# A two-layer decoder trunk on one core: the entry into the second FFN, and the order in which attention copies its accumulators out

## The chip, the cores and the metric

One Trainium2 chip; the program runs on one of its cores. The metric is the time of one execution on the device in microseconds (us). Runs of the kernel before give 2144.81, 2145.89 and 2146.08 us, median 2145.89 us. "Before axis" times below are microseconds from the start of the span in the profiled execution of the kernel before.

## The reference

The trunk has two layers of width 1024 over 1024 positions. Each layer is a mixer and a dense SwiGLU feed-forward part (FFN), each with an RMS norm ahead of it and a residual addition behind it.

```python
for i in range(DEPTH):                       # DEPTH = 2
    h = rms_norm(x, mix_norm[i])
    if i % 2 == 0:
        x = x + short_conv_mixer(h, ...)
    else:
        x = x + dilated_attention_mixer(h, ...)   # 16 heads x 64, 3 dilated branches
    h = rms_norm(x, ffn_norm[i])
    x = x + swiglu(h, w_gate, w_up, w_down)  # (silu(h @ w_gate) * (h @ w_up)) @ w_down
return rms_norm(x, final_norm)
```

Everything is fp32. The RMS norm needs, for each position, the mean over 1024 features of the squares.

## The kernel before

**Numbers and layout.** The residual x lies transposed in SBUF as eight tiles `X[k]` of 128 features x 1024 positions; "first half" and "second half" are columns 0 to 511 and 512 to 1023. An fp32 operand is used as two parts: ScalarE (ACT) copies it to the rounded type fp32r (the high part; L139 for weights, L567 for FFN operands), VectorE (DVE) subtracts that from the operand (the low part; L140, L568). A product is then three matmuls on TensorE (PE): high x high, high x low, low x high. The weight splits stand in one list; `ensure(i)` makes all splits up to number i at that point of the program, `take` hands one out.

**Order.** The order of each engine's instructions is the order in which the program writes them (`manual_schedule`, L103); an engine that waits holds back all that stands behind it. PSUM has eight banks of 128x512, handed out in a ring; a new accumulation waits until what was copied or read from its bank is done.

**FFN.** The FFN's in-projection is done with Strassen's products: a unit (u, m) is product m (1 to 7) of output block u, 12 matmuls of 128x512 each (L575 to L577). `unit_order` (L262) writes the order; in the second FFN (`key` 1) it is, by number n from 0: (0,1) (1,1) (2,1) (3,1) (0,2) (1,2) (2,2) (3,2) (4,1) (4,2) (0,6) (1,6) (0,7) (1,7) (0,4) (1,4) (0,5) (1,5) (0,3) (1,3) (2,6) (2,5) (2,7) (3,6) and so on. `save` (L581) is ACT's copy of a partial from its bank into an SBUF tile `part`; `add` (L585) is DVE's addition of a bank to such a part. `whole` (L613) calls them, and `out` (L1235) finishes a quarter of the output: even units (gate) through Silu on ACT (L1239), odd units (up) by DVE's product with the gate (L1242), then a store from the POOL queue (L741) and, when all four quarters of a block are there, four DVE sums (L749). The quarter (0,0) of blocks 0 to 3 needs only products 1 and 2; `first` adds the bank of product 2 to the part of product 1. Before, the four quarters (0,0) of blocks 0 to 3 are finished behind unit (0,4), number 14.

**The second operand set.** Products 3 to 7 need sums and differences of normalised halves. `second_half` (L1187 and around it) is a generator whose steps make four DVE combinations, or four high parts on ACT (L567) and four low parts on DVE (L568). `feed_forward` calls its steps behind certain unit numbers, `n in (5, 6, 9, 10, 11, 15)` for the second FFN (L1273).

**Entering the FFN.** The attention's out-projection ("ao") produces X[k], first half for k = 0 to 7, then second half for k = 0 to 7, nine matmuls each on lines L369 to L371. DVE adds each bank to X[k] (L506), and `chained` (L448) sums the squares for the norm: ACT squares X[k] (L460 or L467); the sum over k is made in one of two ways. With `by_dma` (the first FFN's norm) k = 0 goes to `acc`, k = 1 to `acc2`, k = 2 to 5 are added by four accumulating DMAs from the POOL queue (L469, even k onto `acc`, odd k onto `acc2`), and DVE adds the square of k = 6, then `acc2`, then the square of k = 7 (L470). Without it (the second FFN's norm) DVE adds all seven (L462). `put_off` holds an addition back by one step. `stats` (L485 to L502) turns the sums into the scale of each position: PE sums over features, ACT a root (L488), DVE a reciprocal and a diagonal (L489, L494), PE spreads it (L501), ACT copies it out (L502). Between the k's, `gained` (L1179, L1183) scales the second half by the gain on ACT and adds four tiles by accumulating DMAs on the POOL queue; ACT's queue spills X[k] to HBM (L1331); SP's queue loads weights (L151).

**Attention.** Heads are worked in pairs p, two heads a. `values` (L1566 on) accumulates output and denominator of one head in two banks, `acc[0]` for the first and `acc[1]` for the second column half. In a loop of j = 0 to 7 ACT copies the denominators (L1598) and outputs (L1599) of `acc[0]` out behind j = 3, of `acc[1]` behind j = 7. Scores (L1503, L1504) of a later head take the freed banks. `finish` (L1601) of the last pair takes logarithm and exponential of the denominators (L1631), multiplies (L1624) and splits the outputs for the out-projection, half by half; the weight splits of the out-projection, 128x384 each ("ao"), follow.

Of the kernel before, what the change touches and what calls it, by code (L numbers as in the profile page):

```python
# [24 lines left out]
NPAIR = H // 2  # L25
# [70 lines left out]
def trunk(ctx: ExitStack, tc: tile.TileContext, x, gains_in, cwi, ck, cwo, wqkv, wo, relb,  # L96
# [8 lines left out]
    def page(name, dt=F32):  # L105
        return pages.tile([128, 1024], dt, name=name, tag="page", bufs=PAGES)
# [3 lines left out]
    def half_page(name, dt=F32):  # L110
        return scope["pool"].tile([128, 512], dt, name=name, tag="half", bufs=scope["halves"])
# [4 lines left out]
    def half(h):  # L116
        return slice(h * HALF, (h + 1) * HALF)
# [45 lines left out]
    def ensure(upto):  # L163
        while op_state[0] < min(upto + 1, len(ops)):
            key = ops[op_state[0] + 1][0] if op_state[0] + 1 < len(ops) else None
            if key in sums_of:
                sums_of.pop(key)()
            if op_state[0] not in made:
                made[op_state[0]] = ops[op_state[0]][1]()
            op_state[0] += 1  # L170
# [223 lines left out]
    class Norm:  # L394
# [57 lines left out]
        def chained(self, k, c0, c1):  # L452

            s = slice(c0, c1)
            if self.acc is None:
                self.acc, self.rstd = page("acc"), page("rstd")
            acc = self.acc[:, s]
            if not self.by_dma and k:
                to = half_page("sq")
                nc.scalar.activation(to, X[k][:, s], AF.Square)  # L460
                self.flush()
                self.put_off = lambda: nc.vector.tensor_tensor(out=acc, in0=acc, in1=to, op=ALU.add)  # L462
                return
            if k == 1:
                self.odd = half_page("acc2")
            to = half_page("sq") if k > 1 else self.odd if k else acc
            nc.scalar.activation(to, X[k][:, s], AF.Square)  # L467
            if 1 < k < 6:
                nc.gpsimd.dma_start(out=(acc, self.odd)[k % 2], in_=to, accum_op=ALU.add)  # L469
            add = lambda t: nc.vector.tensor_tensor(out=acc, in0=acc, in1=t, op=ALU.add)  # L470
            if k > 5:
                self.put_off = lambda: add(to)
            if k == KT - 2:
                self.flush()
                add(self.odd)
                self.odd = None
# [64 lines left out]
    class Strassen:  # L541
# [75 lines left out]
        def whole(self, u, m, d):  # L617

            if m == 1:
                d["p"] = self.bank()  # L620
            elif m in (2, 5):
                d["q" if m == 2 else "r"] = self.bank()
            self.mm((u,), m, d["q" if m == 2 else "r" if m in (5, 3) else "p"], m in (1, 2, 5))
            if m in (1, 6, 7):
                d[{1: "u1", 6: "u2", 7: "u3"}[m]] = self.save(d["p"])
            if (u, m) == (0, 6):
                self.first(0)
            if m == 4:
                self.out(u, (1, 0), d.pop("p"))
            elif m == 3:  # L630
                self.out(u, (0, 1), self.add(d.pop("u2"), d.pop("r")))
            elif m in (5, 7) and "u3" in d and "r" in d:
                self.out(u, (1, 1), self.add(d.pop("u3"), d["r"]))
            early = self.key != 0
            if m == 2 and u > 3 + early or (u, m) in ((0, 4), (3, 7)):
                for x in {0: range(4), 3: (4,) * early}.get(u, (u,)):
                    self.out(x, (0, 0), self.first(x))
                    del self.st[x]["u1"]

# [506 lines left out]
    class Swiglu(Strassen):  # L1146
# [100 lines left out]
        def feed_forward(self, stats, last_step, after, final=None):  # L1247
            prep = []

            def start(n):  # L1250
                if n == 0:
                    last_step()
                    if not self.key:
                        for m in (6, 7):
                            combos[self.key, 1](m)
                        ensure(self.at(3, 1))
                if n == 1 + self.key:
                    next(stats)
                if n == 1:
                    if self.key:  # L1260
                        for m in (6, 7):
                            combos[self.key, 1](m)
                    ensure(self.at(0, 6))
                if n == 2 + 2 * self.key:
                    run(stats)
                    prep.append(self.second_half())
                    next(prep[0])
                    nc.scalar.activation(scratch, eps, AF.Silu)
                if n == 2:
                    ensure(self.at(1, 6))  # L1270
                elif n == 4:
                    ensure(self.at(1, 7))
                if n in ((5, 7, 8, 9, 11), (5, 6, 9, 10, 11, 15))[self.key]:  # L1273
                    ensure(self.base + n + 3)
                    next(prep[0], None)

            self.run(start)
            key = ("d", self.key)
            if final:
                final(key, self.plain, self.hid)  # L1280
                return
            for n in range(KT):
                add_to_x(n, both(take(key + (n,)), self.plain, self.hid))
                after(n)
# [98 lines left out]
    def attention(norm):  # L1383
# [185 lines left out]
        def values(p, a, st):  # L1569
            lf, lh, ld, lp = (st[n] for n in ("lf", "lh", "ld", "lp"))  # L1570
            o, z = st["o"], st["z"]
            n0 = slice(64 * a, 64 * a + 64)
            z0 = slice(64 - 64 * a, 128 - 64 * a)
            acc = [bank(), bank()]
            kd = [[128, 4], [1, 32]]
            b1 = [[32, 16], [1, 8]]

            def mm(ih, off, dims, u, rhs, first=False, last=False):
                nc.tensor.matmul(view(acc[ih], off, dims), vx[:, u, 64 * a:64 * a + 128], rhs,  # L1579
                                 start=first, stop=last)  # L1580

            for ih in range(2):
                for r4 in range(4):
                    mm(ih, r4 * 32, kd, 8 + r4, view(lf, ih * HALF + r4 * 32, kd), first=r4 == 0)
                    if r4 % 2:
                        yield
            for r4 in range(4):
                mm(1, r4 * 32, kd, 12 + r4, view(lh, r4 * 32, kd))
                if r4 % 2:
                    yield  # L1590
            for j in range(8):
                off = (j % 4) * 8
                mm(j // 4, off, b1, j, view(ld, blk(j), b1), last=False)
                if j:
                    mm(j // 4, off, b1, j - 1, view(lp, blk(j), b1), last=j % 4 == 3)
                if j % 4 == 3:
                    ih, s = j // 4, half(j // 4)
                    nc.scalar.activation(z[n0, s], acc[ih][z0], AF.Copy)  # L1598
                    nc.scalar.activation(o[n0, s], acc[ih][n0], AF.Copy)  # L1599
                yield  # L1600

        def finish(p):

            o, z = OZ.pop(p)
            if p < NPAIR - 1:
                zd, rd = zdram[p]
                nc.sync.dma_start(zd, z[0:65:64])
                yield
                zc = scope["pool"].tile([128, 16], F32, name="zc", tag="zc", bufs=2)
                nc.sync.dma_start(zc, bass.AP(zd.tensor, zd.offset, [[16, 128], [1, 16]]))  # L1610
                yield
                nc.vector.reciprocal(zc, zc)
                nc.sync.dma_start(bass.AP(rd.tensor, rd.offset, [[16, 128], [1, 16]]), zc)
                yield
                nc.sync.dma_start(z, bass.AP(rd.tensor, rd.offset, [[S, 2], [0, 64], [1, S]]))
                yield
                put_off.append((p, o, z))
                return

            acts[p] = page("o_hi", F32R), page("o_lo", F32R)  # L1620

            def scaled(c0, c1):
                q = slice(c0, c1)
                nc.vector.tensor_tensor(out=o[:, q], in0=o[:, q], in1=z[:, q], op=ALU.mult)  # L1624

            def parts(h):
                split(o[:, half(h)], [t[:, half(h)] for t in acts[p]])

            nc.scalar.activation(z, z, AF.Ln)
            for h in range(2):  # L1630
                nc.scalar.activation(z[:, half(h)], z[:, half(h)], AF.Exp, scale=-1.0)  # L1631
                scaled(h * HALF, h * HALF + HALF)
                parts(h)
                yield

        def attended():
# [119 lines left out]
        ahead_ao = [k for k, f in ops].index(("ao", 1, 2))  # L1756
# [230 lines left out]
```

## Time and profile before

| what | value |
|---|---|
| runs, median | 2144.81, 2145.89, 2146.08; 2145.89 us |
| profiled execution, its own time | 2144.39 us |
| its span | 2142.6 us (1.79 us of the time lie outside it) |
| mean granted PE clock | 0.997 |
| busy PE / DVE / ACT / POOL | 2120.2 / 1728.1 / 1002.8 / 221.9 us |
| share of the span PE / DVE / ACT / POOL | 99% / 81% / 47% / 10% |
| busy share of the DMA queues: SP and plain hardware queue q1, POOL's software queue q0, ACT's hardware queue q10 | 30.2% / 10.5% / 3.0% |

A matmul's row shows a duration of 0.39 us for 128x512 while the next starts 0.227 us later, since matmuls overlap; a stall is therefore read as the distance of two starts less 0.227. In a row of a timeline stand start, duration, engine, line, operation, written tile and read tile, and in brackets the idle time ahead of it and what ended that. "x4" is a run of four alike, with its whole length.

### The profile page before, as it was taken

To read this page: it belongs to the slowest core of one execution; us is meant where nothing else is said; L and a number is where in the kernel's file an instruction comes from. 1 tells how busy PE (TensorE), PEld (TensorE's weight loads), DVE (VectorE), ACT (ScalarE), POOL (GpSimd) and SP (SyncE) were. 2 spreads that over 40 slices of the span, in tenths; PEclk is the share of its full clock that TensorE was granted. 3 is DMA by queue.
4 is the path that set the end of the run, shared out by engine and by line. 5 is a ranking of instruction groups with operands and counts; after the bars stand their busy time and mean duration, and the time that the engine had idled before them with its cause. 6 is when DMAs were issued, how large, how long until landed. Compare 5 with 4: busy or idle time off the path is not lost.

```text
span 2142.6 us, 30734 instructions
## 1 busy us (share of the span) xinstructions
PE 2120.2 (99%) x11086; PEld 1816.1 (85%) x11086; DVE 1728.1 (81%) x3160; ACT 1002.8 (47%) x1798; POOL 221.9 (10%) x316
## 2 busy tenths in 40 slices
PE   9999999999999999999999999999899999999998
PEld 7788887888888888878999999887788888888887
DVE  8898669888888788864777777868888888978886
ACT  7433336344544444344555555536544444444435
POOL 2000001111212000010111111110011212100000
PEclk9999999999999999999999999999999999999999
DMA  7222643335545784331333333635114544586432
GB/s 214 69 93 69 236 147 94 114 123 172 168 154 181 267 305 141 107 135 52 92 93 94 93 95 83 204 119 185 44 69 156 184 157 166 172 333 217 155 94 79
DMA packets 148067, 306.71 MB, mean 143 GB/s; under 512 B 49851, under 2 KB 61131, under 8 KB 147915
## 3 DMA queue, kind: packets, MB, share of 16 engines
q1 hardware_dynamic: 82026, 206.83, 30.2%
q0 software_dynamic: 25872, 79.02, 10.5%
q10 hardware_dynamic: 40016, 18.90, 3.0%
q8 instruction: 88, 1.44, 0.3%
q14 instruction: 65, 0.52, 0.1%
HBM read 209.06 MB, written 88.28 MB: 139 GB/s over the span
## 4 chain that ended last, share of the span: by engine, by line
PE 77%; issue 10%; DVE 7%; ACT 4%; DMA 2%; POOL 0%; SPq 0%; ACTq 0%; DVEq 0%; POOLq 0%
PE bank L575 16%; PE bank L576 16%; PE bank L577 16%; PE bank L1579 4%; PE bank L371 4%; PE bank L369 4%; PE bank L370 4%; PE bank L670 2%; PE bank L673 2%; PE bank L672 2%; PE bank L1504 1%; PE bank L1503 1%; PE bank L1444 1%; PE bank L1443 1%; PE bank L1442 1%
## 5 line engine op out<-in xcount | busy, mean ns | idle before, releaser
L575 PE MATMUL bank<-b,w 128*128 128x512 f32 x1816 | 710.2, 391 | 6.8 <-ACT part L581 2.8
L576 PE MATMUL bank<-b,w 128*128 128x512 f32 x1816 | 708.1, 390 | 0.5 <-DVE b L916 0.5
L577 PE MATMUL bank<-b,w 128*128 128x512 f32 x1816 | 707.5, 390 | 0.8 <-DVE w L140 0.8
L575 PEld LDWEIGHTS bank<-b,w 128*128 128x128 f32 x1816 | 341.5, 188 | 80.4 <-ACT part L581 3.7
L577 PEld LDWEIGHTS bank<-b,w 128*128 128x128 f32 x1816 | 341.3, 188 | 73.1 <-DVE w L140 1.9
L576 PEld LDWEIGHTS bank<-b,w 128*128 128x128 f32 x1816 | 341.4, 188 | 70.8 <-DVE b L916 1.4
L139 ACT ACTIVATE w<-combo 128x512 fp32r<-128x512 f32 (+2 forms) x448 | 229.1, 540 | 248.6 <-DVE combo L191 227.3
L140 DVE TENSOR_TENSOR w<-combo,w 128x512 fp32r<-128x512 f32 (+2 forms) x448 | 254.8, 582 | 31.5 <-ACT w L139 31.2
L581 ACT ACTIVATE part<-bank 128x512 f32<-128x512 f32 x168 | 100.0, 597 | 294.9 <-PE bank L577 291.2
L140 DVE TENSOR_TENSOR w<-raw,w 128x512 fp32r<-128x512 f32 (+2 forms) x308 | 169.4, 569 | 21.8 <-ACT w L139 21.6
L585 DVE TENSOR_TENSOR part<-part,bank 128x256 f32<-128x256 f32 (+1 forms) x328 | 154.2, 501 | 37.9 <-ACT part L581 21.5
L139 ACT ACTIVATE w<-raw 128x512 fp32r<-128x512 f32 (+2 forms) x308 | 150.8, 527 | 63.2 <-DMA raw<-in_ffn_w_down 18.5
L831 DVE TENSOR_TENSOR x<-x,bank 128x512 f32<-128x512 f32 x168 | 114.8, 684 | 37.1 <-PE bank L577 34.5
L369 PE MATMUL bank<-w_hi,w 128*128 128x512 f32 (+1 forms) x320 | 119.6, 374 | 0.0
L371 PE MATMUL bank<-w_hi,w 128*128 128x512 f32 (+1 forms) x320 | 117.9, 369 | 1.3 <-DVE w L140 1.3
L370 PE MATMUL bank<-w_lo,w 128*128 128x512 f32 (+1 forms) x320 | 117.8, 368 | 0.0
L506 DVE TENSOR_TENSOR x<-x,bank 128x512 f32<-128x512 f32 (+1 forms) x104 | 66.0, 643 | 55.9 <-PE bank L371 48.6
L369 PE MATMUL bank<-h_hi,w_hi 128*128 128x512 f32 x256 | 104.5, 408 | 0.0
L191 DVE TENSOR_TENSOR combo<-raw 128x512 f32<-128x512 f32 (+1 forms) x160 | 103.2, 645 | 0.0
L371 PE MATMUL bank<-h_hi,w_lo 128*128 128x512 f32 x256 | 100.0, 391 | 0.2 <-DVE w_lo L140 0.2
L370 PE MATMUL bank<-h_lo,w_hi 128*128 128x512 f32 x256 | 99.9, 390 | 0.0
L1557 POOL PARTITION_ALL_REDUCE mb<-m x16 | 51.6, 3222 | 395.1 <-DVE m L1554 325.7
(266 smaller groups left out, 3804.4 us busy)
## 6 DMA issues: line engine op xcount, KB each, us to landing
hin<-part SPq DMA_DIRECT2D x126, 256.0 KB
raw<-in_ffn_w_gate SPq DMA_DIRECT2D x44, 512.0 KB
raw<-in_ffn_w_up SPq DMA_DIRECT2D x44, 512.0 KB
b<-ready SPq DMA_DIRECT2D x42, 512.0 KB
part<-sum POOLq DMA_DIRECT2D x72, 256.0 KB, 3.5
raw<-in_ffn_w_down SPq DMA_DIRECT2D x48, 384.0 KB
x<-spill SPq DMA_DIRECT2D x24, 512.0 KB
raw<-in_attn_w_qkv SPq DMA_DIRECT2D x24, 512.0 KB
```

What stands on the lines that cost most here:

```text
L139: nc.scalar.activation(hi, src, AF.Copy)
L140: eng.tensor_tensor(out=lo, in0=src, in1=hi, op=ALU.subtract)
L191: eng.tensor_tensor(out=c, in0=a, in1=b, op=op)
L369: nc.tensor.matmul(b, whi[:, a], ahi[:, s], start=first, stop=False)
L370: nc.tensor.matmul(b, whi[:, a], alo[:, s], start=False, stop=False)
L371: nc.tensor.matmul(b, wlo[:, a], ahi[:, s], start=False, stop=last)
L575: nc.tensor.matmul(b, hi[:, a], bhi, start=start and k == 0, stop=False, skip_group_check=True)
L576: nc.tensor.matmul(b, hi[:, a], blo, start=False, stop=False, skip_group_check=True)
L577: nc.tensor.matmul(b, lo[:, a], bhi, start=False, stop=k == n - 1, skip_group_check=True)
L581: nc.scalar.activation(t, b, AF.Copy)
L585: nc.vector.tensor_tensor(out=t, in0=t, in1=b, op=ALU.add)
L831: nc.vector.tensor_tensor(out=X[n][:, half(h)], in0=X[n][:, half(h)], in1=b, op=ALU.add)
```

## The change

Five edits, all between the attention and the first third of the second FFN:

1. `chained`: for the second FFN's norm the second column half (c0 not 0) takes the branch of the accumulating DMAs; the first half keeps DVE's additions.
2. `whole`: in the second FFN the quarters (0,0) of blocks 0 to 3 are finished behind unit (1,3), number 19, and not behind (0,4), number 14.
3. `feed_forward`: the steps of `second_half` in the second FFN come behind numbers 5, 6, 11, 12, 13, 16 and no more behind 5, 6, 9, 10, 11, 15. The `ensure` beside it moves along.
4. `values`: for all pairs but the last both banks are copied out behind j = 7, `acc[1]` first, then `acc[0]`.
5. `finish`: the split of the fourth "ao" weight is made between the two halves of the last pair's outputs, and not behind both.

```diff
-            if not self.by_dma and k:
+            if not self.by_dma and k and not c0:
...
-            if m == 2 and u > 3 + early or (u, m) in ((0, 4), (3, 7)):
-                for x in {0: range(4), 3: (4,) * early}.get(u, (u,)):
+            if m == 2 and u > 3 + early or (u, m) in ((1, 3) if self.key == 1 else (0, 4), (3, 7)):
+                for x in {u * (u < 2): range(4), 3: (4,) * early}.get(u, (u,)):
...
-                if n in ((5, 7, 8, 9, 11), (5, 6, 9, 10, 11, 15))[self.key]:
+                if n in ((5, 7, 8, 9, 11), (5, 6, 11, 12, 13, 16))[self.key]:
...
-                if j % 4 == 3:
-                    ih, s = j // 4, half(j // 4)
+                for ih in ((j // 4,) * (j % 4 == 3) if p == NPAIR - 1 else (1, 0) * (j == 7)):
+                    s = half(ih)
                     nc.scalar.activation(z[n0, s], acc[ih][z0], AF.Copy)
                     nc.scalar.activation(o[n0, s], acc[ih][n0], AF.Copy)
...
                 parts(h)
+                if h == 0:
+                    ensure(ahead_ao + 1)
```

DVE's order at the end of the second column half of the out-projection (the last steps of `chained`, k = 6 and 7); `acc_13662` is the page `acc2`:

```order
 L506 TENSOR_TENSOR x<-x,bank 128x512
-L462 TENSOR_TENSOR acc<-acc,sq 128x512
+L470 TENSOR_TENSOR acc<-acc,sq 128x512
+L470 TENSOR_TENSOR acc<-acc,acc_13662 128x512
 L1157 SCALAR_TENSOR_TENSOR hcol<-x,gains,rstd 128x512
 L568 TENSOR_TENSOR b<-hcol,b 128x512
 L506 TENSOR_TENSOR x<-x,bank 128x512
-L462 TENSOR_TENSOR acc<-acc,sq 128x512 x2
+L470 TENSOR_TENSOR acc<-acc,sq 128x512
 L1157 SCALAR_TENSOR_TENSOR hcol<-x,gains,rstd 128x512
```

One addition in each of the steps of k = 2 to 5 above these rows is gone as well; here stand additions that read the square made just ahead of them and the page that the DMAs write.

ACT's order behind unit number 9 of the second FFN; `part<-bank` is `save`, `b<-hcol` a step's four high parts:

```order
 L567 ACTIVATE b<-x 128x512 x4
-L581 ACTIVATE part<-bank 128x512
+L581 ACTIVATE part<-bank 128x512 x3
+L139 ACTIVATE w<-raw 128x512
 L567 ACTIVATE b<-hcol 128x512 x4
-L581 ACTIVATE part<-bank 128x512 x2
-L139 ACTIVATE w<-raw 128x512
+L581 ACTIVATE part<-bank 128x512
+L139 ACTIVATE w<-raw 128x512
+L581 ACTIVATE part<-bank 128x512
+L139 ACTIVATE w<-combo 128x512
 L567 ACTIVATE b<-hcol 128x512 x4
```

The four high parts that stood ahead of two copies of partials now stand behind them, and so does the next group.

ACT's order in the attention, where one pair's second head ends; `w_hi<-raw` is a weight split of 128x640:

```order
 L1566 ACTIVATE lp<-lp 128x512
-L139 ACTIVATE w_hi<-raw 128x640
-L1598 ACTIVATE z<-bank 64x512
-L1599 ACTIVATE o<-bank 64x512
-L139 ACTIVATE w_hi<-raw 128x640
+L139 ACTIVATE w_hi<-raw 128x640 x2
+L1598 ACTIVATE z<-bank 64x512
+L1599 ACTIVATE o<-bank 64x512
 L1598 ACTIVATE z<-bank 64x512
 L1599 ACTIVATE o<-bank 64x512
```

The first pair of copies moves down to the second; all four stand together.

## The prediction

> **What bounds the kernel now.** The page first. PE is busy for all but 22 us of the span, so an edit is worth only the PE stalls that it takes away or makes.
>
> ```profile
> span 2142.6 us, 30734 instructions
> PE 2120.2 (99%) x11086; PEld 1816.1 (85%) x11086; DVE 1728.1 (81%) x3160; ACT 1002.8 (47%) x1798; POOL 221.9 (10%) x316
> ```
>
> Next PE's waits, asked for one stretch at a time: attention (960 to 1440), out-projection (1440 to 1480), end of the norm (1480 to 1520), first third of the second FFN (1520 to 1560). Columns: what waited, for whom, us in all, times, longest.
>
> ```profile
> PE bank L1503 <- ACT o L1599: 2.3, 4, 0.6
> ...
> PE bank L371 <- DVE w L140: 1.0, 1, 1.0
> ...
> PE bank L501 <- DVE diag L494: 0.9, 1, 0.9
> ...
> PE bank L575 <- ACT part L581: 2.8, 2, 1.5
> PE bank L575 <- DVE part L585: 1.9, 1, 1.9
> ```
>
> These nine stalls, 8.9 us, are what the five edits aim at. The last stretch costs more than its waits, as the table by windows shows (length, busy PE, PEld, DVE, ACT, POOL; granted clock, DMA share, GB/s):
>
> ```profile
> 1520.00:1560.00 40.00, 35.30 (x147) 28.08 (x146) 36.44 (x59) 19.79 (x35) 3.31 (x6) 0.96 0.09 34
> ```
>
> The clock is 0.96 there. PE's timeline has the place:
>
> ```profile
> 1544.67 0.39 PE L577 MATMUL bank<-b,w 128*128 128x512 f32 x1
> 1546.93 0.47 PE L575 MATMUL bank<-b,w 128*128 128x512 f32 x1 [1.87 <-DVE part L585]
> ...
> 1548.01 0.63 PE L576 MATMUL bank<-b,w 128*128 128x512 f32 x1
> ...
> 1551.34 0.39 PE L575 MATMUL bank<-b,w 128*128 128x512 f32 x1
> ```
>
> The first pair is a stall of 1546.93 - 1544.67 - 0.23 = 2.03 us (0.23 is the distance of two starts in full flow, as between the unit's other matmuls). Behind it eight matmuls take 1551.34 - 1548.01 = 3.33 us where 8 x 0.23 = 1.84 were due: 1.5 us more. So this stall cost 3.5.
>
> **Copies of accumulators (edit 4).** One of the four stalls on PE:
>
> ```profile
> 1072.04 0.40 PE L371 MATMUL bank<-h_hi,w_lo 128*128 128x512 f32 x1
> 1073.02 0.39 PE L1503 MATMUL bank<-qa,ka 128*128 128x256 f32 x1 [0.58 <-ACT o L1599]
> ```
>
> 0.98 - 0.23 = 0.75 us each, 3.0 for four. Freeing the banks in the other order changes which bank the scores get; I take it that all four go. But ACT now makes two pairs of copies where one stood. What a pair takes, and whether that hurts, is read in a slot and behind it:
>
> ```profile
> 1047.73 0.60 ACT L1598 ACTIVATE z<-bank 64x512 f32<-64x512 f32 x1 [2.23 <-PE bank L1579]
> 1048.34 0.59 ACT L1599 ACTIVATE o<-bank 64x512 f32<-64x512 f32 x1
> 1048.83 0.62 ACT L1472 ACTIVATE ka<-kq 64x512 fp32r<-64x512 f32 x1
> ...
> 1062.29 1.05 ACT L1566 ACTIVATE lf<-lf 128x1024 f32<-128x1024 f32 x1
> ...
> 1063.62 1.05 PE L1579 MATMUL bank<-lf,vx 128*128 128x128 f32 x8
> ...
> 1105.93 0.63 ACT L1472 ACTIVATE qb<-kq 64x512 fp32r<-64x512 f32 x1 [1.39 <-POOL mb L1557]
> ```
>
> A pair is 1048.83 - 1047.73 = 1.1 us, and the next head's operands (L1472) start that much later. In this slot ACT has no idle time from there to the exponential, which ends at 1063.34, 0.28 ahead of the PE that reads it; less some 0.06 from end to start, 0.2 of 1.1 is free and 0.9 becomes a stall. In the next slot ACT waits 1.39 on POOL, which swallows the 1.1. I found three slots of the first kind (the copies near 1048, 1155, 1262): 3 x 0.88 = -2.6. Sum **+0.4**, between 0 (one slot more) and +3.0 (DVE's or POOL's share of the chain hides it).
>
> **The "ao" split (edit 5).**
>
> ```profile
> 1459.78 0.39 PE L370 MATMUL bank<-w_lo,w 128*128 128x512 f32 x1
> 1461.15 0.50 PE L371 MATMUL bank<-w_hi,w 128*128 128x512 f32 x1 [0.98 <-DVE w L140]
> ...
> 1458.74 0.69 DVE L140 TENSOR_TENSOR o_lo<-o,o_hi 128x512 fp32r<-128x512 f32 x1 [0.70 <-ACT o_hi L139]
> ```
>
> PE lost 1.37 - 0.23 = 1.14, and 0.1 in the slower start of the next matmul. The split's low part fits into DVE's wait of 0.70 ahead of the second `o_lo`, over two microseconds before PE wants it. **+1.2**; down to +0.7 if ACT's high part, ahead of the second `o_hi`, pushes the latter by its own half microsecond.
>
> **Plain quarters later, high parts behind the copies (edits 2, 3).** What delayed the units (0,7) and (0,3):
>
> ```profile
> 1523.62 2.42 ACT L567 ACTIVATE b<-hcol 128x512 fp32r<-128x512 f32 x4 [2.74 <-DVE hcol L1187]
> 1525.95 1.07 ACT L581 ACTIVATE part<-bank 128x512 f32<-128x512 f32 x2
> ...
> 1543.70 2.49 DVE L568 TENSOR_TENSOR b<-x,b 128x512 fp32r<-128x512 f32 x4
> ```
>
> Copies of partials on ACT, for whose banks PE waits, stand behind four high parts of 0.6 each; ACT was idle 2.74 ahead of those, so the copies can go first. The same holds for the other L581 stall, and DVE's addition L585 stands behind these four low parts likewise. All three stalls go, with the slow matmuls. From the window's row that is 40 - 35.30 = 4.7, and 1.5 of slow flow: 6.2 us. Not all stays: DVE's work there is only moved, and it was idle for no more than 40 - 36.44 = 3.56 us of the window. PE cannot get further ahead of DVE than that. Laying DVE's new order end to end at the 0.60 of its rows, I get new small waits of PE (bank of a gate, operands of (0,3)) and one of some 1.5 near (2,7), where the quarters of blocks 0 to 3 now stand ahead of a weight's low part: gain **+3.1**, between +1.5 (another stall above 2 us with the slow matmuls behind) and +4.7.
>
> The Trainium skill (TensorE: Matmul & The Clock Gate, Part 1) has the clock halve only after an idle window of about 3.4 us; the stall above had 2.03 and slow matmuls behind it, so here the row decides; by the page the slow stretch would not hang on this stall and 1.5 could stay, a gain nearer the lower end.
>
> **DMA sums (edit 1).** DVE's additions go at their distance of 0.60 (two starts):
>
> ```profile
> 1491.99 0.69 DVE L462 TENSOR_TENSOR acc<-acc,sq 128x512 f32<-128x512 f32 x1
> 1492.59 0.75 DVE L1157 SCALAR_TENSOR_TENSOR hcol<-x,gains,rstd 128x512 f32<-128x512 f32 x1
> ...
> 1504.12 0.17 DVE L489 RECIPROCAL r<-r 128x4 f32<-128x4 f32 x1
> ```
>
> DVE reaches that reciprocal without idle time ahead of it, was busy for all of 1485 to 1495 (windows below), and PE's L501 waited 0.9 for its result: 4 x 0.60 = 2.4 us less on the chain. But the additions left now wait, as the first FFN's entry, which has this branch already, shows:
>
> ```profile
> 329.53 0.69 DVE L470 TENSOR_TENSOR acc<-acc,sq 128x512 f32<-128x512 f32 x1 [0.70 <-ACT sq L467]
> 331.37 0.69 DVE L470 TENSOR_TENSOR acc<-acc,acc 128x512 f32<-128x512 f32 x1 [1.14 <-DMA acc<-sq]
> ```
>
> 0.70 and 1.14, and 0.70 again for the last square, which stands right behind its operand: 2.54. If the DMAs land as there, the edit brings 2.4 - 2.54 = -0.1. They need not. The landing times (min/median/max us) of the first entry's eight such DMAs, then of the four accumulating DMAs of the same size (L1183) in the second entry; the square of k = 5; the first of the weight loads and the first L1183; two windows; the DMA queues' shares of 1492.5 to 1496.5:
>
> ```profile
> DMA to landing us min/median/max: 3.2/3.3/4.2
> ...
> DMA to landing us min/median/max: 7.0/7.9/9.0
> ...
> 1489.64 0.63 ACT L460 ACTIVATE sq<-x 128x512 f32<-128x512 f32 x1
> ...
> 1485.60 0.33 SPq L151 DMA_DIRECT2D raw<-in_ffn_w_gate  x1
> ...
> 1492.52 0.88 POOL L1183 DMA_DIRECT2D x<-x  x1 [56.35 <-ACT x L1179]
> ...
> 1485.00:1490.00 5.00, 5.00 (x24) 4.14 (x23) 5.00 (x9) 4.01 (x8) 0.00 (x0) 1.00 0.72 192
> 1490.00:1495.00 5.00, 5.00 (x24) 4.14 (x23) 5.00 (x9) 3.68 (x7) 0.96 (x2) 1.00 1.02 349
> ...
> q1 hardware_dynamic: 236, 0.84, 68.5%
> q10 hardware_dynamic: 255, 0.47, 30.5%
> ```
>
> The DMA of k = 5 can be issued at 1489.64 + 0.63 = 1490.3, between a window with 0.72 of the DMA engines busy and one with 1.02. In the last two rows the software queue moved no packet although POOL had issued at 1492.52: SP's weight loads went first. I take the middle of 3.3 and 7.9, 5.6, which holds DVE 2.3 us longer; DVE has no idle time behind it to make that good. The DMA of k = 3, which must land first since both add to `acc2`, is issued with the first load at 1485.6; at the first entry's slowest, 4.2, it lands at 1489.8 and delays nothing. Term **-2.4**, between -0.1 and -8 (rival 2).
>
> The Trainium skill (DMA: Bandwidth & Descriptors, Queues, rings and completion order) says that each DMA engine takes turns between the queues it has work for. By that the four DMAs would have half the engines and land near 5; the two queue rows show the software queue at nought.
>
> **Sum.** 0.4 + 1.2 + 3.1 - 2.4 = 2.3 us. The profiled execution took 2144.39, its span 2142.6 and 1.79 around it: 2142.1. The median of the runs, 2145.89, is 1.5 above the profiled one: **2143.6**. That is 0.11% faster; about 0.2%, 4.3 us, is what a measurement of this kernel can tell from no change.
>
> **Rivals.**
>
> 1. *The DMAs are on time* (they start before the loads fill the engines; for it 0.72, and no load ahead of 1485.6). Then 0.4 + 1.2 + 3.1 - 0.1 = 4.6, 2141.3, and 2138.7 if the copies cost nothing too. Chance 0.29.
> 2. *The sums come last.* If k = 3 takes 7.9 like L1183, k = 5, which waits for that landing, is issued at 1493.5 and lands at 1501.4, against 1490.3 + 3.3 = 1493.6 on time: DVE stands 7.8 us longer at L470, and with it bank releases, operands and L501. Then 4.7 - 0.1 - 7.8 = -3.2, and 1.5 for slow matmuls behind so long a stall: 4.7 slower, 2150.6. It turns the sum to slower from 4.6 us of lateness on. For it L1183's 7.0 to 9.0; against it that those were issued later and behind one another. Chance 0.18.
> 3. *The stalls only move.* DVE is at 36.44 of 40; if all of edits 2 and 3 comes back as waits for it, and the attention nets 0: 1.2 - 2.4 = -1.2, 2147.1. Against it ACT's idle 2.74. Chance 0.13.
>
> My forecast has 0.40. Faster by over 0.2% (below 2141.6): 0.20 of rival 1 and 0.10 of the forecast, 0.30. Slower by over 0.2% (above 2150.2): 0.11 of rival 2 and 0.02 of the third, 0.13. Within: 0.57. Range 2139.0 to 2149.5: down to rival 1's lower end nearly, up to a lateness of some 5 us with the slow matmuls; 0.05 lies below it and 0.15 above.
>
> **What would show it.** Right: no wait of L1503 on L1599 but about three of L1579 on ACT's exponential, no wait of L371 near 1460, L575 not waiting for L581 ahead of (0,7) and (0,4), clock 1.00 in that window, an `acc` addition on L470 waiting 2 to 5 us for a DMA, and PE waiting about 3 at L501. Wrong: landings of L469 of 3.3 throughout (rival 1), or of 7 and more with PE idle for over 6 us near 1500 (rival 2); the waits on exponentials missing, or in more slots than three; new waits of L575 on DVE that add up to 6 us (rival 3).

## The result, and the profile after

The changed kernel takes 2150.27 us (median of 12 runs, 2149.76 to 2151.21), the kernel before 2145.01 in the same series (12 runs, 2143.47 to 2146.31). The ratio is 1.0026, 95% interval 1.0018 to 1.0034: slower by 0.26%, where 2143.6 and a range up to 2149.5 were forecast. The profiled execution's span went from 2142.6 to 2147.8 us.

PE's waits of the changed kernel, by the same stretches as before (960 to 1440, 1480 to 1520, 1520 to 1560, 1560 to 1600; 1440 to 1480 has none now):

```profile
PE bank L1579 <- ACT lf L1566: 2.4, 3, 0.8
...
PE bank L485 <- DVE acc L470: 7.1, 1, 7.1
...
PE bank L575 <- DVE gate L1242: 0.7, 1, 0.7
PE bank L575 <- ACT b L567: 0.4, 1, 0.4
PE bank L575 <- ACT gate L1239: 0.4, 1, 0.4
PE bank L576 <- DVE b L568: 0.3, 1, 0.3
...
PE bank L577 <- DVE w L140: 1.3, 1, 1.3
```

All nine stalls of before are gone. One new stall of 7.1 us stands at L485, the sum over features for the second half, and it waits for DVE's addition on L470. What DVE waited for there (its timeline, the three additions of the second half):

```profile
1496.06 0.69 DVE L470 TENSOR_TENSOR acc<-acc,sq 128x512 f32<-128x512 f32 x1 [6.97 <-DMA acc<-sq]
1499.81 0.69 DVE L470 TENSOR_TENSOR acc<-acc,acc 128x512 f32<-128x512 f32 x1 [3.06 <-DMA acc<-sq]
...
1503.06 0.69 DVE L470 TENSOR_TENSOR acc<-acc,sq 128x512 f32<-128x512 f32 x1 [0.69 <-ACT sq L467]
```

Ten microseconds for two DMAs. POOL's issues of the four sums (k = 2 to 5) and of the first of the kernel's other accumulating DMAs, then the landing times of the four (min/median/max):

```profile
1480.55 0.88 POOL L469 DMA_DIRECT2D acc<-sq  x1 [44.01 <-PE bank L371]
1484.75 0.85 POOL L469 DMA_DIRECT2D acc<-sq  x1 [3.32 <-ACT sq L467]
1486.40 0.84 POOL L469 DMA_DIRECT2D acc<-sq  x1 [0.80 <-ACT sq L467]
1490.86 0.84 POOL L469 DMA_DIRECT2D acc<-sq  x1 [3.62 <-issue]
1491.41 1.16 POOL L1183 DMA_DIRECT2D x<-x  x1
...
DMA to landing us min/median/max: 3.2/7.2/9.6
```

One by one they landed in 3.19, 5.59, 9.57 and 8.86 us. SP's weight loads, 512 KB each, began at the second of them:

```profile
1484.48 0.33 SPq L151 DMA_DIRECT2D raw<-in_ffn_w_gate  x1
1486.52 0.33 SPq L151 DMA_DIRECT2D raw<-in_ffn_w_up  x1
1487.01 1.63 SPq L151 DMA_DIRECT2D raw<-in_ffn_w_gate  x2
1490.58 6.19 SPq L151 DMA_DIRECT2D raw<-in_ffn_w_up  x2
```

The DMA of k = 4 took 9.57 although it had nothing to wait for but the queues (k = 2, to which it adds, had landed at 1483.7; k = 3 was still under way ahead of it). The one of k = 5 had its square at 1487.9 but was issued at 1490.86, half a microsecond after k = 3 landed (1484.75 + 5.59 = 1490.34), and took 8.86 more. So both slow landings and the chain from k = 3 to k = 5 are seen, and L470 paid for the first before it paid for the second.

Behind the stall PE ran slowly. Its timeline, and the window 1505 to 1510 (length, busy PE, PEld, DVE, ACT, POOL, granted clock):

```profile
1496.30 0.39 PE L577 MATMUL bank<-b,w 128*128 128x512 f32 x1
1503.81 1.87 PE L485 MATMUL bank<-ones,acc 128*128 128x1 f32 x8 [7.12 <-DVE acc L470]
...
1506.11 0.63 PE L576 MATMUL bank<-b,w 128*128 128x512 f32 x1
...
1509.10 0.51 PE L577 MATMUL bank<-b,w 128*128 128x512 f32 x1
...
1505.00:1510.00 5.00, 5.00 (x16) 4.09 (x16) 4.87 (x9) 4.98 (x11) 1.69 (x2) 0.57 0.64 117
```

Where the time went is read by the same matmul in both timelines. Three of them, each as before and then as after: L501 of the first half, L501 of the second half, and the last one behind the moved quarters.

```profile
1478.28 0.70 PE L501 MATMUL bank<-diag,ones 128*128 128x512 f32 x1
1505.07 0.70 PE L501 MATMUL bank<-diag,ones 128*128 128x512 f32 x1 [0.87 <-DVE diag L494]
1559.95 0.39 PE L577 MATMUL bank<-b,w 128*128 128x512 f32 x1
```

```profile
1477.26 0.59 PE L501 MATMUL bank<-diag,ones 128*128 128x512 f32 x1
1512.88 0.70 PE L501 MATMUL bank<-diag,ones 128*128 128x512 f32 x1
1565.04 0.50 PE L577 MATMUL bank<-b,w 128*128 128x512 f32 x1 [1.25 <-DVE w L140]
```

The changed kernel is 1.0 us ahead at the first, 7.8 behind at the second (so 8.8 lost with the DMA sums), 5.1 behind at the third (2.7 won back by the quarters). The 8.8 are DVE's lateness: its three waits above come to 10.72, less 1.80 for three additions of 0.60 that it no longer makes in this stretch, which leaves 8.9. The slow matmuls added next to nothing, for the second half's L501 started at 1512.88 and could not have started before DVE's diagonal ended at 1512.82:

```profile
1512.13 0.69 DVE L494 TENSOR_TENSOR diag<-eye,r 128x512 f32<-128x512 f32 x1
```

### The profile page after: what moved, and what is told of

The parts are those of the page before. It is cut to its first block, busy times and chain, and to the rows that moved or that the text cites. A ratio compares the mean times of both kernels' runs of the same rounds, so it can differ in the third digit from the quotient of the medians.

```text
span 2147.8 us, 30745 instructions
## 1 busy us (share of the span) xinstructions
PE 2120.0 (99%) x11086; PEld 1817.5 (85%) x11086; DVE 1717.2 (80%) x3156; ACT 1001.3 (47%) x1798; POOL 224.6 (10%) x320
## 4 chain that ended last, share of the span: by engine, by line
PE 77%; issue 10%; DVE 5%; ACT 5%; DMA 2%; POOL 0%; SPq 0%; DVEq 0%; POOLq 0%; ACTq 0%
PE bank L575 16%; PE bank L577 16%; PE bank L576 16%; PE bank L1579 5%; PE bank L371 5%; PE bank L369 5%; PE bank L370 5%; PE bank L670 2%; PE bank L673 2%; PE bank L672 2%; PE bank L1504 1%; PE bank L1503 1%; DMA acc<-sq 1%; DVE w L140 1%; DVE combo L191 1%
## 5 line engine op out<-in xcount | busy, mean ns | idle before, releaser
L371 PE MATMUL bank<-w_hi,w 128*128 128x512 f32 (+1 forms) x320 | 117.8, 368 | 0.3 <-DVE w L140 0.3
L371 PE MATMUL bank<-h_hi,w_lo 128*128 128x512 f32 x256 | 100.0, 391 | 0.2 <-DVE w_lo L140 0.2
```

The lines of the kernel that those rows point to most:

```text
L371: nc.tensor.matmul(b, wlo[:, a], ahi[:, s], start=False, stop=last)
```

## The experiments

The theory after the result: the loss is all in the DMA sums, and they are late because SP's six weight loads fill the DMA engines in just that stretch. Rivals: the other edits lose too; ACT's spills, or the sums' waiting for each other, hold them up.

**Edit 1 undone** in the changed kernel:

```diff
-            if not self.by_dma and k and not c0:
+            if not self.by_dma and k:
```

> The changed kernel with the first edit undone: the second half's squares are added by DVE again, edits 2 to 5 stay. Theory (the loss is all in the late DMA sums, 8.9 us between the two traces from 1478 to L501): 2150.3 - 8.9 = about 2141.4 us, 0.17% faster than before, with PE's wait of 7.1 at L485 gone. Rival (the moved quarters and copies lose as well, and DVE would be late there anyway): 2146 or more.

2140.39 us (11 runs) against 2144.65 before; ratio 0.9982 (0.9973 to 0.9991). PE's waits from 1480 to 1520 are those of before again:

```profile
PE bank L501 <- DVE diag L494: 0.9, 1, 0.9
```

The loss is all in the DMA sums, as the theory had it, and edits 2 to 5 together gain 0.18%, 4.3 us.

**Edit 1 alone** in the kernel before (the same line the other way round).

> The kernel before with the first edit alone. Theory (the DMA sums are late by themselves, because of the weight loads of that stretch): 2145.0 + 8.9 = about 2153.9 us, L469's last landings 8 to 10 us. Rival (they are late only because edit 5 brings the out-projection forward against the loads): 2145 to 2148, landings 3 to 6.

2154.03 us (5 runs); ratio 1.0042 (1.0029 to 1.0056), 9.4 us slower. Landing times of the four sums, and DVE's two waits:

```profile
DMA to landing us min/median/max: 3.2/7.0/9.3
...
1497.88 0.69 DVE L470 TENSOR_TENSOR acc<-acc,sq 128x512 f32<-128x512 f32 x1 [6.65 <-DMA acc<-sq]
1501.56 0.69 DVE L470 TENSOR_TENSOR acc<-acc,acc 128x512 f32<-128x512 f32 x1 [2.98 <-DMA acc<-sq]
```

The same picture without the other edits: the earlier out-projection isn't to blame.

**The loads behind the sums.** SP reads a little of `acc2` behind the DMA of k = 5, and so waits for its landing ahead of its loads:

```diff
+    behind = dram.tile([128, 16], F32, name="behind")
...
                 nc.gpsimd.dma_start(out=(acc, self.odd)[k % 2], in_=to, accum_op=ALU.add)
+            if k == 5 and not self.by_dma:
+                nc.sync.dma_start(behind, self.odd[:, 0:16])
```

> The changed kernel, and SP reads 16 columns of acc2 into a scratch tensor behind the DMA of k = 5, so that its six weight loads for the second FFN start only when the sums have landed. Theory (the loads hold the sums up): all landings of L469 3.2 to 4.5 us, no wait of PE at L485, 2141 to 2143.5 us, the loads arriving late being worth up to 2. Rival (the spills on ACT's queue, or the DMAs waiting for each other, hold them up): landings of 6 and more, 2149 to 2152.

2144.55 us (11 runs); ratio 0.9996 (0.9987 to 1.0005). The four landing times, DVE's waits (L473 is L470 here) and PE's (L488 and L504 are L485 and L501):

```profile
DMA to landing us min/median/max: 3.2/4.0/5.0
...
1490.76 0.69 DVE L473 TENSOR_TENSOR acc<-acc,sq 128x512 f32<-128x512 f32 x1 [1.66 <-DMA acc<-sq]
1494.18 0.69 DVE L473 TENSOR_TENSOR acc<-acc,acc 128x512 f32<-128x512 f32 x1 [2.73 <-DMA acc<-sq]
...
PE bank L504 <- DVE diag L497: 2.4, 1, 2.4
PE bank L488 <- DVE acc L473: 1.5, 1, 1.5
```

The landings fell from 5.6, 9.6 and 8.9 to 3.8, 4.3 and 5.0 for k = 3, 4 and 5: the loads are what made them that long. But the time expected was missed by a microsecond, and this kernel is 4.2 us slower than the one without DMA sums (2140.39 in the same series). The DMA of k = 5 still waits for k = 3, and an L1183 follows it at once on its own queue. DVE's waits at the three additions come to 1.66 + 2.73 + 0.69 = 5.08, less 1.80 for the additions saved: 3.3 us late. PE's wait of 2.4 at L501 is this same lateness, not that of the weights, now loaded from 1494.5 on: DVE has no idle time from the last square to the reciprocal ahead of L501.

```profile
1497.43 0.69 DVE L473 TENSOR_TENSOR acc<-acc,sq 128x512 f32<-128x512 f32 x1 [0.69 <-ACT sq L468]
...
1506.30 0.17 DVE L492 RECIPROCAL r<-r 128x4 f32<-128x4 f32 x1
```

From the first half's L501 to the second half's this kernel takes 29.98 us (1477.27 to 1507.25), the kernel before 26.79 and the changed kernel 35.62. So the loads account for 5.6 of the 8.8 us lost; 3.2 are lost without them, and slow matmuls behind that L501 add some 1.5.

**The spills later.** The second half's spills of k = 2 to 7 behind the last square:

```diff
-                nc.scalar.dma_start(spill[n][:, half(j)], X[n][:, half(j)])
+                if j == 0 or i == 0 or n < 2:
+                    nc.scalar.dma_start(spill[n][:, half(j)], X[n][:, half(j)])
...
             norm.flush()
+            for n in range(2 if i else KT, KT):
+                nc.scalar.dma_start(spill[n][:, half(1)], X[n][:, half(1)])
```

> The changed kernel with the second half's spills of k = 2 to 7 issued together behind the last square, so that ACT's queue is empty while the sums run; the weight loads stay. Theory (the loads hold the sums up): the last landings of L469 stay at 6 to 9, 2147.5 to 2150.5 us. Rival (the spills do): landings of 3.2 to 4.5, about 2142.

2152.22 us (5 runs), outside both forecasts; ratio 1.0035 (1.0023 to 1.0048), and landings of 3.18, 4.91, 6.85 and 4.38. It doesn't decide about the spills, since it moved the loads too: four of the six waited for pages that a spill still had to read.

```profile
1487.16 0.33 SPq L151 DMA_DIRECT2D raw<-in_ffn_w_up  x1
1503.42 1.56 SPq L151 DMA_DIRECT2D raw<-in_ffn_w_gate  x2
...
SPq L151 <- DMA spill<-x: 17.6, 4, 15.9
```

So it is a middle step: two loads beside the sums, and k = 4 lands in 6.9, between 4.3 with none and 9.6 with all. What the spills alone cost the sums stays open. The time was lost elsewhere: PE waited 2.0 at the sums and then 5.1 at L501, ahead of which ACT had waited 3.7 for a weight load, and slow matmuls came behind both.

**Only k = 2 and 3 by DMA**, in the changed kernel; DVE adds the rest:

```diff
-            if 1 < k < 6:
+            if 1 < k < (6 if self.by_dma else 4):
...
-            if k > 5:
+            if k > (5 if self.by_dma else 3):
+                self.flush()
                 self.put_off = lambda: add(to)
```

> The changed kernel with accumulating DMAs for k = 2 and 3 alone in the second half; k = 4 to 7 and acc2 are added by DVE. Theory (only the DMAs issued into the weight loads are late, and acc2 is read long after k = 3 lands): landings of L469 3.2 and some 5.6 us, no wait of DVE on a DMA there, two additions fewer than without DMA sums: 2140.4 - 1.0 = about 2139.4 us, 2139 to 2140.5. Rival (any accumulating DMA in this stretch costs DVE a wait): 2143 or more.

2140.74 us (11 runs); ratio 0.9985 (0.9976 to 0.9994). Landings 3.18 and 5.59, no wait on a DMA, as expected; but no better than without DMA sums (2140.39), a miss of 1.3. From the step of k = 3 on DVE has five additions here and six with its own sums, 0.60 less, and it pays that for the square of k = 7:

```profile
1489.25 1.48 DVE L470 TENSOR_TENSOR acc<-acc,sq 128x512 f32<-128x512 f32 x2
1490.77 0.69 DVE L470 TENSOR_TENSOR acc<-acc,acc 128x512 f32<-128x512 f32 x1
...
1494.02 0.69 DVE L470 TENSOR_TENSOR acc<-acc,sq 128x512 f32<-128x512 f32 x1 [0.70 <-ACT sq L467]
```

**Edits 2 and 3 alone** in the kernel before (their diff is above).

> The kernel before with edits 2 and 3 alone. Theory (their gain in the trace of the changed kernel, 2.7 us net of the new waits, doesn't hang on the late sums): 2144.7 - 2.7 = about 2142.0 us, clock 1.00 in the stretch behind 1520. Rival (the late sums hid a part: with DVE on time the moved quarters collide less): 2141 or less; other rival (without edit 1 the stalls come back): 2144 or more.

2142.46 us (11 runs) against 2143.96; ratio 0.9995 (0.9986 to 1.0003): by the times alone unclear. The trace settles the stretch: PE's waits from 1520 to 1600 are those of the changed kernel but for one of 0.4 (here 0.7, 0.4, 0.3 and 1.3), the three old ones are gone, and the matmul of 1559.95 above comes 2.7 us earlier where PE had been 0.4 late ahead of 1520, so 3.0 are gained there. About 1.6 of it is lost again in that execution near 1915, far behind the change, where PE waits twice for ACT's weight splits. The medians differ by 1.5; half of the 3.0 is the slow matmuls of the kernel before, and whether each of its executions has them isn't known (see the last section).

**New order of copies for second heads only**, with edit 1 undone:

```diff
-                for ih in ((j // 4,) * (j % 4 == 3) if p == NPAIR - 1 else (1, 0) * (j == 7)):
+                for ih in ((j // 4,) * (j % 4 == 3) if p == NPAIR - 1 or not a else (1, 0) * (j == 7)):
```

> The changed kernel without the DMA sums (edit 1 undone), and the copies of accumulators in the new order only for the second head of each pair. Theory (the four stalls of L1503 are all at second heads, the three new ones of L1579 all behind first heads): both kinds gone, 2140.4 - 2.5 = about 2137.9 us, 0.3% faster than before. Rival (the banks' ring shifts, and other stalls come): 2139.5 to 2142.

2138.31 us (6 runs) against 2143.96; ratio 0.9969 (0.9958 to 0.9981). PE's only wait from 960 to 1440:

```profile
PE bank L371 <- DVE w_lo L140: 0.2, 1, 0.2
```

Both kinds of stall are gone: the four all lay at second heads, and the three new ones behind first heads. This version beats both kernels. Against the kernel before of its own series it gains 5.65 us, and edits 2 to 5 gained 4.26 in theirs, so 1.4 more, where 2.5 were expected; the traced executions show 3.0 (spans of 2138.3 and 2135.3).

**This and only k = 2 and 3 by DMA.**

> The kernels first_two and second_heads in one: DMA sums for k = 2 and 3 alone, the new order of copies for second heads alone. Theory: the two gains add up, 2144.7 - 4.3 - 2.5 - 1.0 = about 2136.9 us. Rival: no better than second_heads alone.

2138.11 us (7 runs); ratio 0.9970 (0.9959 to 0.9981). No better than the last, as the rival had it.

## Why the prediction was wrong, point by point

- **The mechanism was named, its size and its chance were not.** Rival 2 was the course of things: k = 5 waiting for k = 3, DVE standing at L470 for 10.0 us on DMAs, slow matmuls behind. It gave 2150.6, and 2150.27 was measured; it had a chance of 0.18. That its time came so near is partly luck, for errors in its own working went against each other: k = 3 took 5.6, not 7.9; k = 4, which it left out, took 9.6; DVE's waits on DMAs grew by 8.9 (10.03 against 1.14 in the first entry), not 7.8; and the 1.5 for slow matmuls was not paid on top.
- **The step that failed** is the term of edit 1, "I take the middle of 3.3 and 7.9, 5.6", which made the term -2.4. Measured: -8.8, from L501 to L501. The rows at that very place (7.0 to 9.0 for DMAs of the same size) were the nearer ones; the 3.2 to 4.2 came from an entry in which SP loads nothing. Averaging them against each other hid that they belong to two conditions, and the loads' issue rows told which of the two held from k = 3 on. The experiments split the loss: 5.6 of it goes when the loads move behind the sums, and 3.2 stays, with DVE still waiting 4.4 for the DMAs of k = 4 and 5.
- **The other half of that term** was mis-sized as well. "4 x 0.60 = 2.4 us less on the chain" counted an addition (k = 1) that lay ahead of DVE's unbroken stretch; from there three are gone, 1.8 us. Against the waits of 2.54 edit 1 would have lost some 0.7 even with prompt DMAs; the trial with the first two alone, in which DVE waited for no DMA, gained nothing either.
- **"SP's weight loads went first"** was too much. In the changed kernel the three queues share the stretch from 1490 to 1500 (packets, MB, share of the engines):

```profile
q1 hardware_dynamic: 522, 1.91, 53.5%
q0 software_dynamic: 377, 0.70, 37.9%
q10 hardware_dynamic: 294, 0.52, 13.9%
```

The software queue moves 0.70 MB there beside 2.43 of the others. That agrees with the turns between queues of which the Trainium skill speaks (DMA: Bandwidth & Descriptors, Queues, rings and completion order); but taking turns with two busy queues, and with two or three DMAs of one's own in flight, made landings of 9, and not the 5 that was worked out from it. Why no packet of the software queue moved in the 4 us of the prediction's two rows stays open.
- **Copies of accumulators**: right. +0.4 forecast; all four stalls went, and three new ones stand at L1579, on ACT's exponential as said. Read by the same matmul, each of the four was worth 0.84 and each of the three costs 1.05, with the slow start behind it, +0.2 in all; over the whole attention PE gains 0.5 (0.97 later than before at 1040, 0.44 at 1440).
- **The "ao" split**: right. +1.2 forecast; the stall at L371 is gone and PE goes from 0.44 later than before to 0.84 earlier there, 1.3.
- **Quarters and high parts**: right. +3.1 forecast; 2.7 behind the late sums, 3.0 alone. The new waits came where they were laid out (a gate's bank, operands of (0,3), a weight's low part near (2,7) with 1.3), and the clock in that window was 1.00.
- Rival 1 (DMAs on time) and rival 3 (the stalls only move) are out.

## What to carry to other kernels

A DMA's price is that of the place where it runs: take landing times from the same stretch and the same neighbours on the queues, and where two rows differ, ask what differs between them and don't take the middle. Work moved from a busy engine to a DMA queue saves nothing if the next instruction of that engine waits for it: even with the loads out of the way the DMA sums lost 3.2 us. Count the additions that are left and what each of them will wait for. An edit that removes stalls in one kind of slot and makes them in another (first and second heads) is worth splitting: in the traces PE gained 3.3 us over the attention with the second heads alone (0.15 later than before at 1040, 3.19 earlier at 1440), where the whole netted 0.5.

## What the runs showed of the hardware

The slow matmuls behind a stall of PE came behind shorter gaps than the idle window of about 3.4 us of which the Trainium skill speaks (TensorE: Matmul & The Clock Gate, Part 1): idle times of 1.87 in the kernel before, 1.96 with the spills later and 2.41 with the loads behind were each followed by matmuls 0.43 apart, while idle times of 1.52 (kernel before, at 1533.84), 1.49 (loads behind, ahead of L488) and 1.25 (changed kernel, at 1565.04) were not. Here are the gap without and the gap with it in the loads-behind kernel, and three windows of that trace (length, busy PE, PEld, DVE, ACT, POOL; granted clock, DMA share, GB/s):

```profile
1498.18 1.05 PE L488 MATMUL bank<-ones,acc 128*128 128x1 f32 x8 [1.49 <-DVE acc L473]
...
1507.25 1.13 PE L504 MATMUL bank<-diag,ones 128*128 128x512 f32 x2 [2.41 <-DVE diag L497]
...
1509.07 0.63 PE L578 MATMUL bank<-b,w 128*128 128x512 f32 x1
...
1495.06:1498.48 3.42, 1.93 (x11) 1.32 (x9) 2.73 (x5) 1.83 (x3) 0.84 (x1) 1.00 0.79 256
1505.30:1508.72 3.42, 1.47 (x5) 0.90 (x6) 2.47 (x5) 1.54 (x5) 0.00 (x0) 1.00 1.08 302
1508.72:1512.13 3.41, 3.41 (x10) 2.63 (x9) 2.50 (x4) 2.65 (x5) 0.00 (x0) 0.50 0.30 55
```

The slow stretch is one in which the granted clock is 0.50, and such a stretch is 3.41 us long or a multiple of it: 3.41 in the kernel before (from 1547.82) and here, 10.24 in the changed kernel (from 1499.08), twice 6.83 with the spills later (from 1499.47 and 1513.13). In the trace of edit 1 alone the stretches start at 939.71, 1502.91 and 1557.52, which lie 165 and 16 times 3.413 apart. So in these traces the clock goes by a fixed raster of 3.41 us, and what counts is how idle PE was in the window of the raster just ahead: 1.87 of 3.41 in the kernel before and 1.95 here gave a slow window, 1.52 and 1.49 did not. A slow window after a stall costs some 1.5 us (eight matmuls 0.43 apart instead of 0.23).

It follows that the place of a stall in the raster matters too. The stretch at 939.71 shows it: eight small matmuls (L524, 33x16 operands, 936.4 to 939.0) fill nearly all of the window ahead of it, and the same eight, at other places of the raster, are followed by full clock in the other nine traces. Where between 1.5 and 1.9 us the limit lies, and how small matmuls are counted, stays open; no run varied the gap by itself.
